# Decode of a down projection's output pair emitted ahead of the next weight block's split

## The chip, the cores and the metric

The kernel runs on one core of a Trainium2 chip. The metric is the device time in microseconds (us) of one execution; lower is better. The core's engines work side by side, each through its own queue in order, and wait for each other through semaphores: TensorE (PE; matmul, with weight loads shown apart as PEld), VectorE (DVE), ScalarE (ACT), GpSimd (POOL) and SyncE (SP, which issues most of the DMAs). Matmuls write to PSUM, which has eight banks of 128 x 512 float32; everything else lies in SBUF.

## The reference

A trunk of two layers on a sequence of 512 tokens with 1024 channels. In each layer a token mixer and cross attention add to the residual x, and then a gated MLP with a causal convolution of width 3 does:

```python
def conv_ffn(h, w_up, conv_w, conv_b, w_down):
    u = h @ w_up
    c = conv_general_dilated(u, conv_w[:, None, :], window_strides=(1,),
                             padding=[(CONV_WIDTH - 1, 0)], ...) + conv_b
    a, g = jnp.split(c, 2, axis=-1)
    return (jax.nn.silu(g) * a) @ w_down

x = x + conv_ffn(rms_norm(x, ffn_norm[i]), w_up[i], conv_w[i], conv_b[i], w_down[i])
```

The inner width is 2816. Everything is float32. The change is in the last product, `@ w_down`, and in the addition of its result to x.

## The kernel before

Activations are kept transposed: x is eight tiles `xT[0..7]` of 128 channels x 512 tokens. To keep float32 accuracy with fast matmuls, each operand is split into a high part (a cast, on ACT) and a low part (the rest, a subtraction on DVE), and each product is three matmuls: high x high, high x low, low x high.

The MLP of a layer runs in three parts of 4, 4 and 3 inner pairs (`HALVES`); an inner pair is 256 of the 2816 inner channels. Each part first makes its inner activations ("up": matmul, convolution, gate) and then calls `down`, which adds the part's contribution to x. Output channels are handled in four output pairs c = 0..3 of 2 x 128 channels, so c holds `xT[2c]` and `xT[2c+1]`.

In `down`, most products go by Strassen's scheme in Winograd's form: a 2 x 2 block product is made of seven half-size products in place of eight. `seven(c, m)` emits the seven products for output pair c and inner pair m, 21 matmuls of 128 x 256 (L1358). They accumulate over m in four PSUM banks of pair c (`banks[c]`). After the last m, `decode(c)` adds the banks up in the right combination and adds them to x: one copy on ACT (L1368) and seven additions on DVE (L1369 to L1374, L1376). With four inner pairs the order of PE's work is c,m = (0,0) (0,1) (0,2) (1,0) (1,1) (0,3) (1,2) (1,3), then all of c = 2, then all of c = 3. Since PSUM has eight banks and a pair takes four, c = 2 takes over the banks of c = 0, and c = 3 those of c = 1. PE cannot start a bank before decode has read it.

Weights arrive by DMA in blocks of 128 x 1024 into three `raw` buffers. A block for the seven products carries weights for two inner pairs. POOL makes four sums of its quarters in a `wsum` tile (L285, `block_sums`; two such tiles). `combined` then splits both: ACT casts the raw part (L308) and the sums (L311), DVE makes their low parts (L309 and L312). The split block lies in two buffers each of `whi` and `wlo`, of which there are six each, so three such blocks are alive at a time. Blocks of ordinary products are split in L257 and L260.

Who asks for the next block: `emitted(c, m)` (L1347) is called when PE's matmuls of (c, m) have been emitted. After each odd m the block of that pair is done with: `release` counts its buffers as free and `refill` makes the next blocks in the plan of all weights, at most two pieces ahead (a piece is the weights of one output pair, or one half of an up projection). `make_block` emits the split, the POOL sums of the block after it and the DMA of a later one. So the last `emitted` of a pair, at m = nq - 1, emits a split, and `decode(c)` is called right after it.

PE runs in the order in which the code emits. The other engines are ordered by the framework's planner: it simulates the program with costs of its own and lets each engine take the earliest emitted instruction that is ready in its simulation. The order it finds is then fixed, and on the chip each engine's queue runs in that order. `tc.issue_after(ins)` ties what is emitted inside it: each instruction on the engine of `ins` is put behind `ins` in that engine's queue.

Of the kernel before, what the change touches and what calls it, by code (L numbers as in the profile page):

```python
# [85 lines left out]
def _pieces():  # L86
# [3 lines left out]
    def piece(key, name, i, ks, *ranges):  # L90
        plan.append((key, name, i, ks, ranges))

    for l in range(2):
# [24 lines left out]
        for nq in HALVES:  # L118
            for q in range(base, base + nq):
                for key, c in ((("ua", l, q), 256 * q), (("ug", l, q), DFF + 256 * q)):  # L120
                    piece(key, "w_up", l, (6, 7, 4, 5, 0, 1, 2, 3) if key in SEVEN else K8, (c, c + 256))
            for c in range(4):
# [14 lines left out]
    return out  # L137


SEVEN = [("ua", l, q) for l in range(2) for q in (5, 6, 8, 9)] + [("ug", 0, 9)]  # L140
SUMS_AT = {1:(4,5),2:(0,1),3:(2,3)}
TURNS = ('mm', 'mm', 'sm', 'sm', 'lg', 'lg', 'tp', 'tp')

# [41 lines left out]
def trunk(ctx, tc, head_d, x_t, mem_t, wpack, cols_a_d, cols_d, conv_d, gate_d, rel_bias, diff_lambda, consts, onehot, out):  # L185
    nc = tc.nc
    mm = nc.tensor.matmul
    V, A, G = nc.vector, nc.scalar, nc.gpsimd
# [9 lines left out]
    def bank(tag):  # L198
        return ps.tile([128, 512], F32, name=f"ps_{tag}", tag=tag)
# [12 lines left out]
    def blk(b, w=128):  # L212
        return slice(w * b, w * b + w)
# [108 lines left out]
    def by_seven(i):  # L322
        return plan[i][0][0] == "dn" or plan[i][0] in SEVEN

# [76 lines left out]
    def product(p, parts, n, pairs, ids=None, total=None):  # L401
        ids = range(len(parts)) if ids is None else ids
        total = len(parts) if total is None else total
        first, last = (ids[0], ids[-1]) if len(ids) == total else (0, total - 1)
        for i in ids:
            (hi, lo), (bh, bl) = parts[i], pairs[i]
            mm(p, hi[:, blk(n)], bh, start=i == first, stop=False)  # L407
            mm(p, hi[:, blk(n)], bl, start=False, stop=False)  # L408
            mm(p, lo[:, blk(n)], bh, start=False, stop=i == last)  # L409
# [65 lines left out]
    first = [bank("mm"), bank("mm"), bank("sm"), bank("sm")]  # L475
# [25 lines left out]
    with tc.tile_pool(name="ini", bufs=1) as ip, tc.manual_schedule(engines={E.Activation, E.DVE, E.Pool, E.SP}):  # L501
# [57 lines left out]
        for k in range(KT):  # L559
# [19 lines left out]
            full, left, right = slice(0, S), blk(0, S // 2), blk(1, S // 2)  # L579
# [588 lines left out]
    def ffn(pool, l, acc):  # L1168
# [5 lines left out]
        left, right = blk(0, 256), blk(1, 256)  # L1174

        def take(n):
            nb[0] += n
            return [bank(TURNS[i % 8]) for i in range(nb[0] - n, nb[0])]

        def refill():  # L1180
            nonlocal live
            while done[0] < min(len(order), first_of[min(used[0] + 2, len(plan))]) and live + sizes[done[0]] <= WB:
                live += sizes[done[0]]
                make_block()

        def begin(key):
            nonlocal live
            assert plan[used[0]][0] == key, (plan[used[0]][0], key)
            used[0] += 1
            refill()  # L1190
            return used[0] - 1

        def whole_piece(i):
            nonlocal live
            while done[0] < first_of[i + 1]:
                live += sizes[done[0]]
                make_block()
            assert live <= WB
            return made[i]

        def release(i, n, all_of_it=False):
            nonlocal live
            live -= n
            if all_of_it:
                made[i] = None
            refill()

        def ctile():
            return pool.tile([128, S], F32, name="cvo", bufs=7)
# [64 lines left out]
        def mid_tile():  # L1274
            return xs.tile([128, S], F32R, name="mid", tag="xs", bufs=XS)
# [62 lines left out]
        def down(base, nq, mids, pairs, last, acc2):  # L1338
            first = used[0]
            whole = [plan[first + c][0][0] == "dw" for c in range(4)]  # L1340
            banks, seen = {}, [set() for _ in range(4)]

            def start(c):
                begin(("dw" if whole[c] else "dn", l, base, c))
                banks[c] = take(2 if whole[c] else 4)

            def emitted(c, m):  # L1347
                if m == nq - 1 or m % 2:
                    release(first + c, 1 if whole[c] else 2, m == nq - 1)

            def seven(c, m, some=steps):
                while len(made) <= first + c or len(made[first + c]) <= m:
                    refill()
                for i in some:
                    b, h = place[i]
                    (hi, lo), (bh, bl) = made[first + c][m][i], mids[m][i]
                    for t, (w, v) in enumerate(((hi, bh), (hi, bl), (lo, bh))):
                        mm(banks[c][b][:, h], w, v, start=b not in seen[c], stop=m == nq - 1 and t == 2 and i in close)  # L1358
                        seen[c].add(b)
                if some[-1] != steps[-1]:  # L1360
                    return
                emitted(c, m)
                if m == nq - 1:
                    decode(c)

            def decode(c):
                b, x1, x2, u, y = banks[c], xT[2 * c], xT[2 * c + 1], ctile(), ctile()[:, left]
                A.copy(u[:, left], b[2][:, left])  # L1368
                V.tensor_add(x1, x1, b[0])  # L1369
                V.tensor_add(y, u[:, left], b[2][:, right])  # L1370
                V.tensor_add(u[:, right], y, b[1][:, right])
                V.tensor_add(y, y, b[3][:, left])
                V.tensor_add(x2, x2, b[1])
                V.tensor_add(x1, x1, u)  # L1374
                x2v = x2.rearrange("p (h c) -> p h c", h=2)
                V.tensor_add(x2v, x2v, y.unsqueeze(1).to_broadcast([128, 2, 256]))  # L1376
                if last and l == 1:
                    for n in (2 * c, 2 * c + 1):
                        nc.sync.dma_start(out[n], xT[n])

            def eight(c, n, m0, m1, total=nq):
                parts = whole_piece(first + c)
                product(banks[c][n], parts, n, pairs, range(2 * m0, 2 * m1), 2 * total)

            if all(whole):
                for c0 in (0, 2):
                    cs = (c0, c0 + 1)
                    for c in cs:
                        start(c)
                        for n in range(2):  # L1390
                            eight(c, n, 0, nq - 1)
                        emitted(c, 1)
                    for c in cs:
                        for n in range(2):
                            eight(c, n, nq - 1, nq)
                            update(2 * c + n, banks[c][n], lambda k: c_attn(1, k), acc2)
                            nc.sync.dma_start(xres[2 * c + n], xT[2 * c + n])
                        emitted(c, nq - 1)
                return
            own, mixed = steps[:3], steps[3:]  # L1400
            seq = [(0, m, steps) for m in range(nq - 1)] + [(1, 0, steps)]
            if nq > 3:
                seq += [(1, 1, steps), (0, nq - 1, steps)] + [(1, m, steps) for m in range(2, nq)]
            else:
                seq += [(0, nq - 1, own), (1, 1, own), (0, nq - 1, mixed), (1, 1, mixed), (1, 2, steps)]
            seq += [(c, m, steps) for c in ((2,) if whole[3] else (2, 3)) for m in range(nq)]
            for c, m, some in seq:
                if c not in banks:
                    start(c)
                seven(c, m, some)  # L1410
            if whole[3]:
                start(3)
                eight(3, 0, 0, nq)
                V.tensor_add(xT[6], xT[6], banks[3][0])
                nc.sync.dma_start(out[6], xT[6])
                eight(3, 1, 0, nq - 1, nq - 1)
                V.tensor_add(xT[7], xT[7], banks[3][1])
                for t, p, queue in zip((left, right), take(2), (nc.sync, nc.scalar)):
                    p = p[:, :S // 2]
                    parts = made[first + 3]  # L1420
                    product(p, parts[-2:], 1, [(bh[:, t], bl[:, t]) for bh, bl in pairs[-2:]])
                    V.tensor_add(xT[7][:, t], xT[7][:, t], p)
                    queue.dma_start(out[7, :, t], xT[7][:, t])

        base, acc2 = 0, None
        for part, nq in enumerate(HALVES):
            mids, pairs = [], []
            last = part == len(HALVES) - 1
            for q in range(base, base + nq):
                c2, ops, at, cs = [], [], {}, {}  # L1430

                def half(key, n, j):
                    if n == 0:
                        at[key] = begin((key, l, q))
                        if (key, l, q) in SEVEN:
                            cs[key] = [conv(p, j + i) for i, p in enumerate(up_by_seven(at[key]))]
# [5 lines left out]
                for n in range(2):  # L1442
                    ua = half("ua", n, 2 * q)
                    ug = half("ug", n, 22 + 2 * q)
# [11 lines left out]
                    else:  # L1456
                        m = mid_tile()
# [104 lines left out]
```

## Time and profile before

| | |
|---|---|
| median of 3 runs | 1151.06 us (1149.73 to 1151.46) |
| the profiled execution | 1149.61 us, of it the span 1147.8 us |
| PE busy | 1139.8 us (99% of the span) |
| DVE, ACT, POOL busy | 932.1, 618.8, 279.3 us |
| granted TensorE clock | 1.000 |
| steps of decode: L1368 / L1369 / L1376 | 19 times each; 373, 676 and 685 ns (median) |

The span is the time from the first to the last instruction; the rest of the profiled time lies around it. Matmuls are pipelined and their ends are modelled, so a busy PE is not PE at its peak: whether PE lost time is read from the starts of its matmuls. A row of the timeline gives start, duration, engine, line, operation, output tile <- input tiles, shapes and the count; in square brackets stands how long the engine was idle before it, and what ended that wait.

### The profile page before, as it was taken

The page shows a single profiled execution, that of the slowest core. Times are in us where ns is not written, and L with a number is a line of the kernel's source. Part 1 is how long each engine was busy: PE and PEld are TensorE (multiplying, and loading weights), DVE is VectorE, ACT ScalarE, POOL GpSimd, SP SyncE. Part 2 cuts the span into 40 slices and gives each one's busy share as a digit, 9 for nine tenths or more (in the row PEclk, how much of TensorE's full clock was granted, in tenths as well). Part 3 has the DMA queues.
Part 4 walks back from the last instruction along what each step waited for, and adds up shares of the span by engine and source line. Part 5 has one row for each costly group of instructions (what it writes and reads, how often), then busy time and mean ns, then how long its engine had stood idle before and what let it go on. Part 6 is the DMA issues. An engine that isn't in the chain of part 4 may idle for free.

```text
span 1147.8 us, 17525 instructions
## 1 busy us (share of the span) xinstructions
PE 1139.8 (99%) x6554; PEld 993.0 (87%) x6554; DVE 932.1 (81%) x1553; ACT 618.8 (54%) x1097; POOL 279.3 (24%) x326
## 2 busy tenths in 40 slices
PE   9999999999999999999999999999999999999998
PEld 7888888888899888999888888988888989899888
DVE  8576778689998899899777637777898888989987
ACT  6676686556553355444557634535655435544542
POOL 0000000004374425760000000000246432575240
PEclk9999999999999999999999999999999999999999
DMA  8522242133314332343252230334222343234312
GB/s 297 166 78 91 79 142 70 60 110 91 111 57 131 108 92 75 92 129 111 87 180 71 96 99 11 96 126 123 74 89 77 94 128 92 91 93 129 107 50 101
DMA packets 39666, 117.87 MB, mean 103 GB/s; under 512 B 4767, under 2 KB 7256, under 8 KB 39582
## 3 DMA queue, kind: packets, MB, share of 16 engines
q1 hardware_dynamic: 39150, 116.37, 32.7%
q8 instruction: 51, 0.84, 0.3%
q10 hardware_dynamic: 432, 0.39, 0.1%
q14 instruction: 33, 0.27, 0.1%
HBM read 112.54 MB, written 4.21 MB: 102 GB/s over the span
## 4 chain that ended last, share of the span: by engine, by line
PE 95%; POOL 2%; DVE 1%; ACT 1%; issue 1%; DMA 0%; SPq 0%; POOLq 0%; ACTq 0%
PE ps_mm L407 6%; PE ps_mm L408 6%; PE ps_mm L409 6%; PE ps_mm L385 6%; PE ps_mm L387 6%; PE ps_mm L386 6%; PE ps_sm L408 4%; PE ps_sm L409 4%; PE ps_sm L407 4%; PE ps_lg L1358 4%; PE ps_mm L1358 3%; PE ps_tp L1358 3%; PE ps_tp L224 3%; PE ps_lg L1233 3%; PE ps_tp L408 3%; PE ps_tp L407 3%
## 5 line engine op out<-in xcount | busy, mean ns | idle before, releaser
L260 DVE TENSOR_TENSOR wlo<-raw,whi 128x1024 fp32r<-128x1024 f32 (+5 forms) x165 | 185.8, 1137 | 75.3 <-ACT whi L257 73.6
L257 ACT CAST whi<-raw 128x1024 fp32r<-128x1024 f32 (+5 forms) x165 | 157.0, 967 | 103.0 <-PE ps_mm L408 20.2
L285 POOL TENSOR_TENSOR wsum<-raw 128x256 f32<-128x256 f32 (+1 forms) x112 | 99.5, 909 | 119.9 <-DMA raw<-in_wpack_dram 71.6
L385 PE MATMUL ps_mm<-whi,xsh 128*128 128x512 f32 (+2 forms) x328 | 126.2, 385 | 0.0
L387 PE MATMUL ps_mm<-whi,xsl 128*128 128x512 f32 (+2 forms) x328 | 123.0, 375 | 0.0
L386 PE MATMUL ps_mm<-wlo,xsh 128*128 128x512 f32 (+2 forms) x328 | 122.8, 374 | 0.0
L407 PE MATMUL ps_mm<-xsh,whi 128*128 128x512 f32 x294 | 115.5, 393 | 0.0
L408 PE MATMUL ps_mm<-xsl,whi 128*128 128x512 f32 x294 | 114.6, 390 | 0.0
L409 PE MATMUL ps_mm<-xsh,wlo 128*128 128x512 f32 x294 | 114.5, 389 | 0.0
L312 DVE TENSOR_TENSOR wlo<-wsum,whi 128x1024 fp32r<-128x1024 f32 (+1 forms) x56 | 69.0, 1232 | 15.2 <-ACT whi L311 15.0
L1286 POOL TENSOR_TENSOR cvo<-cvo 128x256 f32<-128x256 f32 x56 | 47.4, 865 | 134.5 <-DVE cvo L1450 133.4
L407 PE MATMUL ps_sm<-xsh,whi 128*128 128x512 f32 x202 | 78.6, 389 | 0.0
L408 PE MATMUL ps_sm<-xsl,whi 128*128 128x512 f32 x202 | 78.6, 389 | 0.0
L409 PE MATMUL ps_sm<-xsh,wlo 128*128 128x512 f32 x202 | 78.6, 389 | 0.0
L311 ACT CAST whi<-wsum 128x1024 fp32r<-128x1024 f32 (+1 forms) x56 | 53.5, 956 | 36.5 <-POOL wsum L285 29.5
L385 PEld LDWEIGHTS ps_mm<-whi,xsh 128*128 128x128 f32 x328 | 61.7, 188 | 11.4 <-issue 1.0
L387 PEld LDWEIGHTS ps_mm<-whi,xsl 128*128 128x128 f32 x328 | 61.7, 188 | 11.3
L386 PEld LDWEIGHTS ps_mm<-wlo,xsh 128*128 128x128 f32 x328 | 61.8, 188 | 10.1
L1263 POOL MEMSET xsh<- 128x128 f32 x2 | 0.4, 210 | 276.4 <-PE ps_sm L408 190.1
L409 PEld LDWEIGHTS ps_mm<-xsh,wlo 128*128 128x128 f32 x294 | 55.2, 188 | 11.6
L407 PEld LDWEIGHTS ps_mm<-xsh,whi 128*128 128x128 f32 x294 | 55.2, 188 | 11.3 <-issue 0.3
L408 PEld LDWEIGHTS ps_mm<-xsl,whi 128*128 128x128 f32 x294 | 55.3, 188 | 11.2 <-DVE xsl L366 0.4
(446 smaller groups left out, 3167.8 us busy)
## 6 DMA issues: line engine op xcount, KB each, us to landing
raw<-in_wpack_dram SPq DMA_DIRECT2D x178, 512.0 KB, 3.6
xt<-in_x_t_dram SPq DMA_DIRECT2D x15, 256.0 KB, 5.2
raw<-in_wpack_dram SPq DMA_DIRECT2D x15, 256.0 KB, 2.9
raw<-in_wpack_dram SPq DMA_DIRECT2D x8, 384.0 KB, 3.4
xres<-xt SPq DMA_DIRECT2D x8, 256.0 KB, 3.3
xt<-xres SPq DMA_DIRECT2D x8, 256.0 KB, 6.8
out_dram<-xt SPq DMA_DIRECT2D x7, 256.0 KB, 2.0
bt<-bias_d SPq DMA_DIRECT2D x6, 256.0 KB, 4.0
```

Source lines behind the costliest of these rows:

```text
L257: ins = A.copy(hi[:, c], raw[:, c])
L260: V.tensor_sub(lo[:, c], raw[:, c], hi[:, c].bitcast(F32))
L285: tc.keep_in_program_order(getattr(G, "tensor_" + op)(o, x, y))
L311: A.copy(h1[:, m], wsum[:, m])
L312: V.tensor_sub(l1[:, m], wsum[:, m], h1[:, m].bitcast(F32))
L385: mm(p, sh[k][:, blk(b)], hi, start=k == 0, stop=False)
L386: mm(p, sh[k][:, blk(b)], lo, start=False, stop=False)
L387: mm(p, sl[k][:, blk(b)], hi, start=False, stop=k == KT - 1)
L407: mm(p, hi[:, blk(n)], bh, start=i == first, stop=False)
L408: mm(p, hi[:, blk(n)], bl, start=False, stop=False)
L409: mm(p, lo[:, blk(n)], bh, start=False, stop=i == last)
L1358: mm(banks[c][b][:, h], w, v, start=b not in seen[c], stop=m == nq - 1 and t == 2 and i in close)
```

## The change

In the last step of an output pair (m = nq - 1), in the parts that are not the layer's last, `decode(c)` is emitted first, and `emitted(c, m)` after it. What `emitted` puts on ACT is tied behind the first copy of decode, and what it puts on DVE behind decode's last addition. This concerns the parts with four inner pairs, two in each layer, with four decodes each: 16 decodes. The third decode-using place, the last part of the second layer, keeps its order. `SEVEN`, a list of keys made by a comprehension, is written out as a tuple with the same nine keys.

```diff
-SEVEN = [("ua", l, q) for l in range(2) for q in (5, 6, 8, 9)] + [("ug", 0, 9)]
+SEVEN = (('ua', 0, 5), ('ua', 0, 6), ('ua', 0, 8), ('ua', 0, 9), ('ua', 1, 5), ('ua', 1, 6), ('ua', 1, 8), ('ua', 1, 9), ('ug', 0, 9))
...
                 if some[-1] != steps[-1]:
                     return
-                emitted(c, m)
-                if m == nq - 1:
-                    decode(c)
+                if m < nq - 1 or last:
+                    emitted(c, m)
+                    if m == nq - 1:
+                        decode(c)
+                    return
+                with ExitStack() as stack:
+                    for ins in decode(c):
+                        stack.enter_context(tc.issue_after(ins.ins))
+                    emitted(c, m)
 
             def decode(c):
                 b, x1, x2, u, y = banks[c], xT[2 * c], xT[2 * c + 1], ctile(), ctile()[:, left]
-                A.copy(u[:, left], b[2][:, left])
+                first = A.copy(u[:, left], b[2][:, left])
...
-                V.tensor_add(x2v, x2v, y.unsqueeze(1).to_broadcast([128, 2, 256]))
+                final = V.tensor_add(x2v, x2v, y.unsqueeze(1).to_broadcast([128, 2, 256]))
                 if last and l == 1:
                     for n in (2 * c, 2 * c + 1):
                         nc.sync.dma_start(out[n], xT[n])
+                return first, final
```

## The prediction

> **What bounds the kernel now.** I read the page's busy table and chain first, then the waits of TensorE (PE), and then the four down projections that the change touches, engine by engine, in the timeline. The span is 1147.8 us and PE is busy for 1139.8 of it:
>
> ```profile
> PE 1139.8 (99%) x6554; PEld 993.0 (87%) x6554; DVE 932.1 (81%) x1553; ACT 618.8 (54%) x1097; POOL 279.3 (24%) x326
> ...
> PE 95%; POOL 2%; DVE 1%; ACT 1%; issue 1%; DMA 0%; SPq 0%; POOLq 0%; ACTq 0%
> ```
>
> 95% of the chain that ended last is PE. So the time falls only where PE stands still, and what any other engine does costs nothing until PE waits for it. This is who PE waits for:
>
> ```profile
> PE ps_tp L1358 <- DVE cvo L1370: 1.7, 2, 0.8
> PE ps_sm L1358 <- DVE cvo L1370: 1.6, 2, 1.2
> ```
>
> The columns are the total in us, the number of waits and the longest. These are the longest waits of PE, and the only ones after the start of the kernel: four, one in each of the four down projections with four inner pairs, always for L1370, a step of decode on VectorE (DVE). Why DVE is late shows in its timeline in the second of the four (layer 0):
>
> ```profile
> 470.40 1.21 DVE L312 TENSOR_TENSOR wlo<-wsum,whi 128x1024 fp32r<-128x1024 f32 x1
> 471.54 0.94 DVE L309 TENSOR_TENSOR wlo<-raw,whi 128x768 fp32r<-128x768 f32 x1
> 475.71 1.37 DVE L312 TENSOR_TENSOR wlo<-wsum,whi 128x1024 fp32r<-128x1024 f32 x1 [3.23 <-ACT whi L311]
> 477.00 0.41 DVE L1370 TENSOR_TENSOR cvo<-cvo,ps_tp 128x256 f32<-128x256 f32 x1
> ...
> 479.65 1.23 DVE L1376 TENSOR_TENSOR xt<-xt,cvo 128x512 f32<-128x512 f32 x1
> 480.80 1.49 DVE L309 TENSOR_TENSOR wlo<-raw,whi 128x768 fp32r<-128x768 f32 x1
> 482.22 1.76 DVE L312 TENSOR_TENSOR wlo<-wsum,whi 128x1024 fp32r<-128x1024 f32 x1
> 483.91 0.67 DVE L1369 TENSOR_TENSOR xt<-xt,ps_mm 128x512 f32<-128x512 f32 x1
> 484.50 0.41 DVE L1370 TENSOR_TENSOR cvo<-cvo,ps_sm 128x256 f32<-128x256 f32 x1
> ...
> 486.81 0.69 DVE L1376 TENSOR_TENSOR xt<-xt,cvo 128x512 f32<-128x512 f32 x1
> ```
>
> DVE works its queue in order. The split of the next weight block (L309 at 471.54, L312 at 475.71) stands ahead of L1370, and DVE sits idle for 3.23 us before L312, with decode behind it. What L312 waits for, and whether decode was ready, show ScalarE (ACT) and GpSimd (POOL):
>
> ```profile
> 469.92 0.37 ACT L1368 COPY cvo<-ps_tp 128x256 f32<-128x256 f32 x1
> 470.52 0.83 ACT L308 CAST whi<-raw 128x768 fp32r<-128x768 f32 x1 [0.23 <-PE ps_tp L1358]
> 474.63 1.05 ACT L311 CAST whi<-wsum 128x1024 fp32r<-128x1024 f32 x1 [3.27 <-POOL wsum L285]
> 475.58 0.37 ACT L1368 COPY cvo<-ps_sm 128x256 f32<-128x256 f32 x1
> ```
>
> ```profile
> 473.05 0.73 POOL L285 TENSOR_TENSOR wsum<-wsum,raw 128x256 f32<-128x256 f32 x1
> ...
> 475.96 1.71 POOL L285 TENSOR_TENSOR wsum<-wsum,raw 128x256 f32<-128x256 f32 x1
> ```
>
> L312 needs L311, and L311 needs POOL's four sums, which end at about 474.6. Decode's copy (L1368) was over at 470.29. So decode was ready some 7 us before it ran, held by a split that was itself waiting. On PE it looks so:
>
> ```profile
> 476.44 0.28 PE L1358 MATMUL ps_lg<-mid,wlo 128*128 128x256 f32 x1
> 477.56 0.48 PE L1358 MATMUL ps_tp<-mid,whi 128*128 128x256 f32 x2 [0.84 <-DVE cvo L1370]
> 477.87 0.28 PE L1358 MATMUL ps_tp<-mid,wlo 128*128 128x256 f32 x1
> 477.99 0.40 PE L1358 MATMUL ps_tp<-mid,whi 128*128 128x256 f32 x2
> 478.22 0.28 PE L1358 MATMUL ps_tp<-mid,wlo 128*128 128x256 f32 x1
> 478.61 0.47 PE L1358 MATMUL ps_lg<-mid,whi 128*128 128x256 f32 x2
> 478.92 0.28 PE L1358 MATMUL ps_lg<-mid,wlo 128*128 128x256 f32 x1
> ```
>
> and undisturbed, in the chain, nine matmuls take 1.08 us, 0.12 us each from start to start:
>
> ```profile
> 479.56 1.08 PE ps_lg L1358 x9
> ```
>
> **The change part by part.** SEVEN as a tuple holds the same nine keys and is only asked "is this key in it": it emits nothing, 0.
>
> The move itself adds and removes no instruction. It emits the decode of an output pair before the weight block that this pair's last step frees, and ties that block's ACT and DVE instructions behind decode's first copy and last addition. It acts on 4 decodes in each of 4 down projections.
>
> *ACT.* The tie asks for L1368 before the casts. The rows have that order already (L1368 at 469.92, L308 at 470.52): 0.
>
> *DVE, first decode (c = 0).* L1370 to L1376 move ahead of L309 and L312 of the block freed there. They can start when L1368 is over (470.29) and when the earlier block's L312 is off DVE (471.54, where the row of the next instruction starts). (L1369, the first addition, ran before these rows already.) These six take 486.81 + 0.69 - 484.50 = 3.0 us, and 479.65 + 1.23 - 477.00 = 3.88 beside a busy POOL. So they end at 474.5 to 475.4, and PE, which wants the bank at 476.44 + 0.12 = 476.56, finds the whole decode finished; both of its stops here go. Their size: 477.56 - 476.56 = 1.00, then 477.87 - 477.56 - 2 x 0.12 = 0.07, 478.61 - 478.22 - 0.12 = 0.27 (the second bank, which decode reads last in L1373) and 478.92 - 478.61 - 0.24 = 0.07: 1.41 us. In the other three the first stop is
>
> ```profile
> 349.32 0.28 PE L1358 MATMUL ps_mm<-mid,wlo 128*128 128x256 f32 x1
> 349.95 0.35 PE L1358 MATMUL ps_sm<-mid,whi 128*128 128x256 f32 x1 [0.35 <-DVE cvo L1370]
> ...
> 900.41 0.28 PE L1358 MATMUL ps_mm<-mid,wlo 128*128 128x256 f32 x1
> 901.89 0.36 PE L1358 MATMUL ps_sm<-mid,whi 128*128 128x256 f32 x1 [1.20 <-DVE cvo L1370]
> ...
> 1028.38 0.28 PE L1358 MATMUL ps_lg<-mid,wlo 128*128 128x256 f32 x1
> 1029.50 0.36 PE L1358 MATMUL ps_tp<-mid,whi 128*128 128x256 f32 x1 [0.84 <-DVE cvo L1370]
> ```
>
> 0.51, 1.36 and 1.00 by the same subtraction. (The waits put it lower, 0.35 to 1.20, since they count a matmul's modelled end as work; start to start is what the end of the kernel feels.) I take the 0.41 that follows from the case shown for all four. Sum: 1.00 + 0.51 + 1.36 + 1.00 + 4 x 0.41 = 5.5 us.
>
> *What is late next.* The moved split (L309, L312) starts at 474.5 to 475.4 in place of 471.54. L309 takes 0.94 to 1.49, L312 cannot start before L311 ends (475.68) anyway and takes 1.37 to 1.76: it ends at 477.1 to 478.7, before at 477.08. PE needs this block two steps of 21 matmuls (seven products of three) after 476.56, at 476.56 + 42 x 0.12 = 481.6. Cover about 3 us, cost 0. If the cover went, each us beyond it would cost one us in each of the four.
>
> *Second decode (c = 1).* It too goes ahead of a split (that at 480.80). Seven instructions, 483.91 to 487.50, are 3.6 us (4.5 with POOL busy). From 477.1 to 478.7, and not before its copy (475.58 + 0.37), they end at 480.7 to 483.2; the split after them takes 0.94 + 1.37 to 1.49 + 1.76 and ends at 483.0 to 486.4. It is due after 84 matmuls, at 486.6: covered, but at the worst end by 0.2 only.
>
> *Third and fourth decode.* Behind them go splits of the next up projection's weights. When the third decode starts, the fourth pair still takes 84 matmuls (10.1 us), so the 3.6 us of the third are covered. What goes behind the fourth is not the next weight piece but the one after it: 0 as well; uncovered, each would cost at most its 3.6.
>
> *Queues.* Decode issues no DMA in these four, so SP's weight loads keep their order. A weight buffer comes free up to about 3.9 us later (L309 from 471.54 to about 475.4), and so does the load into it; that load serves a block three later, not due in this pair: 0. POOL's sums have no tie. They wait for L312 to free their buffer, which moves by 0 to 1.6 us: under the same covers.
>
> POOL and DVE do get in each other's way: L1376 took 1.23 beside POOL (at 479.65) against 0.69 (at 486.81), and POOL's sums took 1.71 beside DVE against 0.73 with DVE idle. Decode now runs where POOL's sums had DVE idle; two additions from SBUF can hold up the sums by about 2 x 0.7 = 1.4 us. L311 then ends at 477.1, L312 at 478.5 to 478.8: inside the cover of 481.6, but it pushes the second decode's split towards 486.6.
>
> The Trainium skill has a rule that speaks against the move here ("SBUF — State Buffer", section "Who interferes with whom"): a DVE instruction with both inputs in SBUF and a GpSimd instruction that reads SBUF exclude each other for their whole length. The rows agree in kind, but they show a stretch of 0.5 us for L1376 (1.23 against 0.69); by the rule as by the rows the sum stays 5.5, and only the second split's margin suffers.
>
> *The sum.* The profiled execution took 1149.61 us (span 1147.8 and 1.81 around it); less 5.5 it is 1144.1. The median of the runs is 1151.06, 1.45 above it; less 5.5 it is **1145.6 us**, 0.48% less. A change of 0.2% (2.3 us) is about the least that can be told from none.
>
> **The rivals.**
>
> *A new wait at the second split (partial gain).* If POOL's hindrance and the long durations meet, the block due at 486.6 is late by up to 1.4 - 0.2 = 1.2 us in each projection; four such take back up to 4.8 of the 5.5. With half of it, 0.8 each, 3.2 is lost: 1148.8. For it: the worst sum has only 0.2 us. Against it: the short durations leave 3.6.
>
> *Decode is not pulled forward, but the split is pushed back (slower).* The planner that orders ACT, DVE and POOL may leave L1370 to L1376 where they are (477.00 to 480.88), while the tie sends L309 and L312 behind them: L312 ends at 480.88 + 0.94 + 1.37 = 483.2 to 484.1, due at 481.6, so 1.6 to 2.5 us are lost in each besides the old stop: 4 x 2 = 8, 1159. It decides once L1376 ends later than 481.6 - 2.3 = 479.3. Against it: the copy was ready at 470.29 and nothing else stands on DVE between 471.54 and 475.71.
>
> *No change.* PE stops at the same place for something else, such as the first block's split. Its L312 (470.40) is over at 471.6, 5 us before it is due, so I see no candidate: 1151.
>
> **How the numbers follow.** Full gain 0.76 (1145.6); partial 0.08 (1148.8, half of it beyond 0.2%); no change 0.06; slower 0.10 (1159). Faster 0.76 + 0.04 = 0.80, same 0.06 + 0.04 = 0.10, slower 0.10. PE has no other wait to lose, so the low end is the fastest run, 1149.73, less 5.5 and 0.7 for reading errors: 1143.5. The high end takes in the partial case with most of its loss, 1150.0. That leaves out the slower case and half of no change.
>
> **What would show it.** Right: no PE wait on L1370 is left, the six decode instructions stand directly behind the L312 near 470 with no idle of 3.2 us before the next L312, and PE's matmuls at the start of the third pair are 0.12 apart. Wrong: PE or its weight loads waiting on L309 or L312 two or four steps later, L1376 ending after the third pair starts, or POOL's sums ending more than 3 us later than now.

## The result, and the profile after

| | before | after |
|---|---|---|
| median of 6 executions | 1150.29 us (1149.54 to 1151.46) | 1144.29 us (1144.10 to 1145.39) |
| the profiled execution | 1149.61 us | 1144.21 us |
| its span | 1147.8 us | 1142.4 us |

The ratio is 0.9948, with a 95% interval of 0.9936 to 0.9961. The kernel became 6.0 us faster by the medians and 5.4 us by the two profiled executions. In the later sessions below, the median of before was 1149.50 to 1149.83 us, so 5.4 is the nearer figure.

The code grew above `decode`, so the line numbers of after are shifted: the copy L1368 is now L1374, the first addition L1369 is L1375, L1370 to L1373 are L1376, L1377, L1378 and L1379, L1374 is L1380, and the last addition L1376 is L1382. L1376 is thus the last step of decode in the rows of before, and the second in the rows of after.

The page of after, with the busy table, the chain that ended last by engine, and one group of instructions (total and mean busy time, then the idle time before them and what ended most of it):

```profile
PE 1137.8 (100%) x6554; PEld 992.9 (87%) x6554; DVE 934.7 (82%) x1553; ACT 619.8 (54%) x1097; POOL 279.5 (24%) x326
...
PE 99%; DMA 0%; DVE 0%; issue 0%; SPq 0%; ACT 0%
...
L312 DVE TENSOR_TENSOR wlo<-wsum,whi 128x1024 fp32r<-128x1024 f32 (+1 forms) x56 | 67.1, 1198 | 7.1 <-ACT whi L311 5.6
```

The last row in the page of before:

```profile
L312 DVE TENSOR_TENSOR wlo<-wsum,whi 128x1024 fp32r<-128x1024 f32 (+1 forms) x56 | 69.0, 1232 | 15.2 <-ACT whi L311 15.0
```

The chain is now 99% PE, and DVE, ACT and POOL, which held 4% of it between them, are down to nothing or nearly so. The instruction counts of all engines are the same as before. DVE's idle time in front of L312 fell from 15.2 to 7.1 us: DVE stands still less in the place where decode was queued behind it. The waits of PE in after (total us, number, longest):

```profile
PE ps_tp L512 <- PEq L1524: 0.8, 1, 0.8
PE ps_mm L586 <- DVE wlo L260: 0.3, 1, 0.3
PE ps_mm L586 <- ACT xsh L365: 0.2, 1, 0.2
```

The four waits for decode (1.7 + 1.6 us) are gone, and nothing has come in their place: these three belong to the start of the kernel. Measured from start to start of PE's matmuls at L1358, before lost 5.50 us and after 0.00.

The same place as in the prediction, the second of the four projections (layer 0), in the timeline of DVE after:

```profile
469.46 1.21 DVE L312 TENSOR_TENSOR wlo<-wsum,whi 128x1024 fp32r<-128x1024 f32 x1
470.60 0.41 DVE L1376 TENSOR_TENSOR cvo<-cvo,ps_tp 128x256 f32<-128x256 f32 x1
...
473.27 1.23 DVE L1382 TENSOR_TENSOR xt<-xt,cvo 128x512 f32<-128x512 f32 x1
474.42 1.49 DVE L309 TENSOR_TENSOR wlo<-raw,whi 128x768 fp32r<-128x768 f32 x1
475.83 1.76 DVE L312 TENSOR_TENSOR wlo<-wsum,whi 128x1024 fp32r<-128x1024 f32 x1
...
480.77 1.22 DVE L1382 TENSOR_TENSOR xt<-xt,cvo 128x512 f32<-128x512 f32 x1
481.92 0.95 DVE L309 TENSOR_TENSOR wlo<-raw,whi 128x768 fp32r<-128x768 f32 x1
482.79 1.21 DVE L312 TENSOR_TENSOR wlo<-wsum,whi 128x1024 fp32r<-128x1024 f32 x1
```

and of PE after:

```profile
475.50 0.28 PE L1358 MATMUL ps_lg<-mid,wlo 128*128 128x256 f32 x1
475.62 0.40 PE L1358 MATMUL ps_tp<-mid,whi 128*128 128x256 f32 x2
```

The decode starts as soon as the L312 of the earlier block is off DVE. It is over at 473.27 + 1.23 = 474.50, and PE takes the bank at 475.62, 0.12 us after the matmul before it. Before, PE wanted the bank at 476.56 and got it at 477.56. (After reaches this place 0.94 us earlier, because the first projection has already gained its 0.51 + 0.41.) No idle time stands in front of the L312 at 475.83.

The sums of POOL, and the cast that needs them, in after:

```profile
468.21 3.07 POOL L285 TENSOR_TENSOR wsum<-raw 128x256 f32<-128x256 f32 x2 [4.96 <-ACT whi L308]
471.24 0.74 POOL L285 TENSOR_TENSOR wsum<-wsum,raw 128x256 f32<-128x256 f32 x1
472.06 0.74 POOL L285 TENSOR_TENSOR wsum<-raw,wsum 128x256 f32<-128x256 f32 x1
```

```profile
472.83 1.05 ACT L311 CAST whi<-wsum 128x1024 fp32r<-128x1024 f32 x1 [2.42 <-POOL wsum L285]
```

The sums still end late, at 472.80, and the cast L311 still waits for them. What has changed is only who stands behind that wait on DVE. Compared queue by queue, the order of the instructions is the same in both kernels on PE, ACT, POOL and SP; only DVE's differs.

### The profile page after: what moved, and what is told of

Its sections match the earlier page's. It is cut to its first block, busy times and chain, and to the rows that moved or that the text cites. A ratio compares the mean times of both kernels' runs of the same rounds, so it can differ in the third digit from the quotient of the medians.

```text
span 1142.4 us, 17519 instructions
## 1 busy us (share of the span) xinstructions
PE 1137.8 (100%) x6554; PEld 992.9 (87%) x6554; DVE 934.7 (82%) x1553; ACT 619.8 (54%) x1097; POOL 279.5 (24%) x326
## 4 chain that ended last, share of the span: by engine, by line
PE 99%; DMA 0%; DVE 0%; issue 0%; SPq 0%; ACT 0%
PE ps_mm L407 6%; PE ps_mm L408 6%; PE ps_mm L409 6%; PE ps_mm L385 6%; PE ps_mm L387 6%; PE ps_mm L386 6%; PE ps_lg L1358 5%; PE ps_sm L407 4%; PE ps_sm L408 4%; PE ps_sm L409 4%; PE ps_mm L1358 4%; PE ps_tp L1358 4%; PE ps_sm L1358 3%; PE ps_tp L224 3%; PE ps_lg L1233 3%; PE ps_tp L408 3%
## 5 line engine op out<-in xcount | busy, mean ns | idle before, releaser
L311 ACT CAST whi<-wsum 128x1024 fp32r<-128x1024 f32 (+1 forms) x56 | 53.6, 957 | 49.3 <-POOL wsum L285 43.7
L1286 POOL TENSOR_TENSOR cvo<-cvo 128x256 f32<-128x256 f32 x56 | 47.4, 866 | 134.3 <-DVE cvo L1457 133.2
L312 DVE TENSOR_TENSOR wlo<-wsum,whi 128x1024 fp32r<-128x1024 f32 (+1 forms) x56 | 67.1, 1198 | 7.1 <-ACT whi L311 5.6
L387 PEld LDWEIGHTS ps_mm<-whi,xsl 128*128 128x128 f32 x328 | 61.7, 188 | 11.3
L407 PEld LDWEIGHTS ps_mm<-xsh,whi 128*128 128x128 f32 x294 | 55.3, 188 | 11.3 <-issue 0.3
```

The source lines that it names most:

```text
L311: A.copy(h1[:, m], wsum[:, m])
L312: V.tensor_sub(l1[:, m], wsum[:, m], h1[:, m].bitcast(F32))
L387: mm(p, sl[k][:, blk(b)], hi, start=False, stop=k == KT - 1)
```

## Experiments

All are compared with the kernel before on the same chip. Line numbers are those of each kernel.

**The first decode alone, and the other three alone.** The theory says that only the decode of the first output pair (c = 0) is worth anything, since PE waits there and nowhere else. The rival is that each of the four decodes brings its part. Two kernels split the change between them.

```diff
-                if m < nq - 1 or last:
+                if m < nq - 1 or last or c != 0:
```

> Only the first decode (c = 0) of each of the four projections is moved and tied; the decodes of c = 1, 2, 3 keep their old place. Theory (the gain is the first decode alone, since only there PE waited): the whole gain, 1144.3 us, ratio to the kernel before 0.995, no PE wait on decode. Rival (each of the four moved decodes brings its part, through buffers that come free earlier): about a quarter of it, 1148.8 us, ratio 0.999.

Measured: 1144.14 us (1144.06 to 1144.43), ratio 0.9952 (0.9938 to 0.9965). This is the whole gain. PE has no wait at L1358 left.

```diff
-                if m < nq - 1 or last:
+                if m < nq - 1 or last or c == 0:
```

> The counterpart: the decodes of c = 1, 2, 3 are moved and tied, the first keeps its old place. Theory: no gain, 1150.3 us, ratio 1.000, and the four PE waits of 0.35 to 1.2 us on L1376 (the renumbered L1370) are all there, behind the idle of about 3.2 us before L312. Rival: three quarters of the gain, 1145.8 us, ratio 0.996.

Measured: 1149.79 us, ratio 1.0000 (0.9992 to 1.0009), the time of before. PE's waits in this kernel are those of before, under the new line number of the same step:

```profile
PE ps_tp L1358 <- DVE cvo L1376: 1.7, 2, 0.9
PE ps_sm L1358 <- DVE cvo L1376: 1.6, 2, 1.2
```

So 4 of the 16 moved decodes carry the gain, and the other 12 are worth nothing that can be measured.

**The order without the tie.** Is it enough to emit decode first, or must the split be tied behind decode's last addition?

```diff
-                with ExitStack() as stack:
-                    for ins in decode(c):
-                        stack.enter_context(tc.issue_after(ins.ins))
-                    emitted(c, m)
+                decode(c)
+                emitted(c, m)
```

> Decode is emitted first as in the change, but nothing is tied behind it. The planner then puts the freed block's L309 between decode's second and third DVE step, and its L312 still behind decode. Theory (what matters is that no waiting L312 stands ahead of decode): the full gain, 1144.3 us, ratio 0.995, since L309 delays the rest of decode by 0.9 to 1.5 us and there are 2 us to spare. Rival (the tie is needed): the old waits are back, 1149 to 1150 us.

Measured: 1143.84 us (1143.61 to 1144.27), ratio 0.9952 (0.9939 to 0.9964). DVE's timeline in the same place:

```profile
470.20 0.41 DVE L1376 TENSOR_TENSOR cvo<-cvo,ps_tp 128x256 f32<-128x256 f32 x1
470.53 1.16 DVE L309 TENSOR_TENSOR wlo<-raw,whi 128x768 fp32r<-128x768 f32 x1
471.61 0.41 DVE L1377 TENSOR_TENSOR cvo<-cvo,ps_lg 128x256 f32<-128x256 f32 x1
...
473.58 1.23 DVE L1382 TENSOR_TENSOR xt<-xt,cvo 128x512 f32<-128x512 f32 x1
474.73 1.76 DVE L312 TENSOR_TENSOR wlo<-wsum,whi 128x1024 fp32r<-128x1024 f32 x1
```

Now L309, which needs no sums, slips in between two steps of decode, but L312, which does, stays behind them. That is enough: the gain comes from decode standing ahead of the one instruction that waits for POOL, not from its standing ahead of the whole split. The tie is not needed here. This kernel, after, and the one with the first decode alone cannot be told apart by their times.

**A later sum, in both kernels.** If before lost its time because decode was queued behind a split that waited for POOL, then sums that end later must cost before the same again, and after nothing. The first sum of the block whose wait holds decode is made three times (with the same result), which adds two sums to POOL in each of the four projections. It is done in the kernel before and in the kernel after.

```diff
-        g_sums((("add", s1, a21, a22), ("sub", s3, a11, a21), ("sub", s2, s1, a11), ("sub", s4, a12, s2)))
+        g_sums((("add", s1, a21, a22),) * (3 if plan[order[done[0]][0]][0][0] == "dn" and plan[order[done[0]][0]][0][3] == 2 and plan[order[done[0]][0]][0][2] < 8 and done[0] - first_of[order[done[0]][0]] == 1 else 1) + (("sub", s3, a11, a21), ("sub", s2, s1, a11), ("sub", s4, a12, s2)))
```

> The kernel before, with the first of POOL's four sums of one block made three times over (the same result): the block whose split stands ahead of the first decode, in each of the four projections. All other queues keep their order. Two more sums of 0.74 to 1.1 us each, so L311 and L312 come 1.5 to 2.2 us later. Theory (the first decode, and PE behind it, hang on these sums): each us of it is lost on PE in each of the four, 6 to 9 us more, 1156 to 1159 us. Rival (POOL's delay is hidden, PE waited for the amount of DVE work): 1150.3 to 1152 us.

> The same two extra sums per projection in the changed kernel. Theory (the first decode no longer hangs on POOL; the late block has about 2 to 3 us of cover): 1144.3 us, at most 1146, so that the gap to the kernel before with the same extra sums is 12 to 15 us. Rival (the change only moved the wait, its cover is used up already): 6 us or more slower than the changed kernel, 1150 us.

Measured: before with the extra sums takes 1158.33 us (ratio 1.0076, 1.0063 to 1.0090), after with them 1145.76 us (ratio to the plain before 0.9966, 0.9954 to 0.9979). The same work on POOL costs 8.8 us in the one and 1.5 us in the other. PE's waits in before with the extra sums:

```profile
PE ps_tp L1358 <- DVE cvo L1370: 4.6, 2, 2.3
PE ps_sm L1358 <- DVE cvo L1370: 4.5, 2, 2.6
```

Its DVE, in the second projection:

```profile
480.06 1.34 DVE L312 TENSOR_TENSOR wlo<-wsum,whi 128x1024 fp32r<-128x1024 f32 x1 [4.73 <-ACT whi L311]
```

DVE's idle time ahead of L312 grew from 3.23 to 4.73 us, by 1.50. The four stops of PE grew from 0.51, 1.00, 1.36 and 1.00 to 1.99, 2.47, 2.81 and 2.48, by 1.45 to 1.48 each: what POOL is late by goes to PE one for one, through a split that PE does not need yet. These 5.9 us leave 2.9 of the 8.8 open; they are the clock, below. The gap between the two kernels is 12.6 us, as the theory had it (12 to 15). In after with the extra sums, the L312 of the same place waits 0.30 us, decode is long over by then, and no wait for decode appears. Of its 1.5 us, PE shows 1.3 from start to start at L1358. About 0.3 of that is the split of the second decode, whose L312 now ends just too late for the fourth pair in the third and fourth projection (0.1 and 0.2 us), so a little of the rival is true as well. The larger part, 1.0, is one stop elsewhere, in the last part of layer 1:

```profile
PE ps_tp L1358 <- DVE mid L1279: 0.7, 1, 0.7
```

It measures 0.88 us from start to start, and 0.10 more at the next matmul. DVE there runs some 2 us later against PE than in after, and L1279 with it; where DVE first falls behind was not found.

**Where the missing 2.9 us went.** The view of stretches, for the 3 us behind the stops of before with the extra sums. The columns are the stretch, its length, the busy time of PE, PEld, DVE, ACT and POOL, then the granted TensorE clock, the DMA share and the GB/s:

```profile
351.60:355.00 3.40, 3.38 (x16) 3.40 (x17) 3.40 (x6) 1.05 (x1) 3.32 (x5) 0.53 0.01 5
481.80:485.00 3.20, 3.12 (x15) 3.15 (x16) 3.20 (x5) 1.05 (x1) 3.12 (x5) 0.52 0.02 9
908.70:912.00 3.30, 3.24 (x17) 3.27 (x18) 3.30 (x6) 1.05 (x1) 3.22 (x5) 0.57 0.02 9
1038.70:1042.00 3.30, 3.14 (x24) 2.99 (x25) 3.30 (x6) 1.05 (x1) 3.22 (x5) 1.00 0.04 16
```

After three of the four stops the clock was granted at about half for 3 us, and PE did 15 to 17 matmuls in place of 24. After the fourth, which was no shorter (2.48 us), it stayed at 1.00. Does the surplus come from the clock, or does POOL's delay itself cost PE more than it is long? The kernel before with one extra sum in place of two (`* (2 if` in the same line) was to tell.

> The kernel before with one extra sum per projection in place of two. With two, the stops of PE grew from 0.51, 1.00, 1.36, 1.00 us to 1.99, 2.47, 2.81, 2.48, by 1.48 each, but the time grew by 8.8 us and not 5.9; behind three of the four stops the granted TensorE clock stood near one half for some 3 us. Theory A (one for one, and a stop of some 2 us or more can also cost the clock): stops grow by 0.74 each to 1.25, 1.74, 2.10 and 1.74; with the clock unharmed 1152.5 us, with one or two places at the half clock (about 1 us each) 1153.5 to 1154.5. Theory B (the surplus of 2.9 us came from more DVE and POOL work being late, not from the clock): 1154 us with the clock at 1.00 in all four places.

Measured: 1155.64 us (1152.37 to 1157.59), ratio 1.0046 (1.0033 to 1.0059). The stops are 1.34, 1.71, 2.08 and 1.73, on average 0.75 longer than before, about the length of one sum (0.74 us): one for one, as with two. The executions spread over 5 us, and they are ordered by their mean clock: 1152.37 at 1.000, 1154.19 at 0.999, 1155.59 and 1155.69 at 0.997, 1157.15 and 1157.59 at 0.996. The one that kept its full clock took 2.5 us more than before (1149.83), against 0.75 x 4 = 3.0. The rest is the clock. In the profiled execution (1155.69) it fell to one half after two of the four stops, from 905.57 to 908.97 us and from 1035.28 to 1038.68. The rows show the stretches around the second stop (at 479.07, 1.71 us), which kept its clock, and around the third (at 904.18, 2.08 us), which did not:

```profile
475.49:478.89 3.40, 2.02 (x17) 1.82 (x16) 1.66 (x2) 2.05 (x3) 3.40 (x4) 1.00 0.48 148
478.90:482.31 3.41, 3.14 (x24) 2.99 (x25) 3.38 (x7) 1.05 (x1) 3.33 (x5) 1.00 0.02 6
902.16:905.56 3.40, 1.37 (x10) 1.13 (x10) 3.17 (x6) 1.58 (x4) 3.32 (x4) 1.00 0.52 154
905.57:908.97 3.40, 3.40 (x19) 3.40 (x18) 3.40 (x4) 0.62 (x1) 3.32 (x4) 0.50 0.00 0
908.98:912.38 3.40, 3.40 (x30) 3.40 (x30) 3.37 (x5) 1.79 (x2) 0.50 (x1) 1.00 0.48 154
```

1155.69 - 1152.37 = 3.3 us for two such places, about 1.6 each, which is more than the one microsecond I had taken. Counted from start to start within the one execution, they are 1.4 each; with two extra sums they are 1.0 each, since there the slow stretch began while PE still stood. With that the account nearly closes: at L1358 PE loses 14.3 us with two sums, 11.3 with one and 5.5 in before, which is 8.8 and 5.8 more, and the spans of the profiled executions are 9.2 and 6.0 longer. The surplus is thus spent in the slow stretches, as in theory A.

**How much cover the moved split has.** The change pushes the split of the next block behind decode. Extra additions on DVE behind the first decode (`u` added to itself, which nobody reads afterwards) push it further, by two or by five additions of 0.68 to 1.23 us each.

```diff
-                return first, final
+                return first, [final, *(V.tensor_add(u, u, u) for _ in range(2 if not last and c == 0 else 0))][-1]
```

> The changed kernel with two additions on DVE behind the first decode in place of five. The planner lets one step of the second decode go ahead of the tied split as well, so this split comes 1.8 to 2.6 us later, with 2.7 to 3.1 us of cover in the changed kernel; the second decode's split comes 1.2 to 2.0 us later, with about 1.6 us of cover. Theory (these covers, read from the changed kernel's trace, are what there is): no stop at the first split, at the second 0 to 0.4 us in each projection, 1144.3 to 1146 us. Rival (any delay of the splits reaches PE): 4 x 2 us more, 1152 us.

Measured: 1145.99 us (1145.26 to 1146.51), ratio 0.9964 (0.9952 to 0.9976). PE does not stop for the first split. At the second it loses 0.2 us in the second projection and 0.3 in the third from start to start, too little to show among the waits, and within the 0 to 0.4 that was expected. Most of the 1.7 us over after is again in the last part of layer 1, a stop of 1.03 us that after does not have (again put down to L1279), so this run bounds the cover without giving a clean price.

With `range(5 ...)` in the same line:

> The changed kernel with five additions from SBUF to SBUF (0.69 us each, 0.60 from start to start, on a tile that nobody reads again) on DVE behind the first decode and ahead of the split that is tied to it. The planner lets four or five steps of the second decode go ahead of that split too, so it comes 4.7 to 7 us later. In the changed kernel it ends 2.7 to 3.1 us before PE needs it. Theory (that cover is all there is): PE loses 1.8 to 4 us in each of the four, 7 to 16 more, about 1153 us, with PE waiting at the third step of c = 2. Rival (cover is larger since PE waits for something else as well): 1144 to 1147 us.

Measured: 1153.66 us (1153.61 to 1154.51), ratio 1.0038 (1.0025 to 1.0050): slower than before. The largest of PE's waits, and PE's timeline in the second projection:

```profile
PE ps_lg L1358 <- DVE wlo L312: 1.8, 4, 0.5
PE ps_mm L1358 <- DVE wlo L312: 1.8, 4, 0.5
```

```profile
482.89 0.39 PE L1358 MATMUL ps_lg<-mid,wlo 128*128 128x256 f32 x1 [0.44 <-DVE wlo L309]
...
484.02 0.39 PE L1358 MATMUL ps_lg<-mid,wlo 128*128 128x256 f32 x1 [0.52 <-DVE wlo L312]
```

Each projection now stops 1.2 to 1.6 us at its third step and 0.5 at the start of the fourth pair. In all PE loses 9.6 us from start to start (0.6 of it in the last part of layer 1), and 1144.2 + 9.6 = 1153.8 is about the time measured. The cover is real and finite, and the whole gain hangs on it.

**Take the wait away and leave the order.** If the split's wait for the sums is the cause, decode may stay behind it as long as the sums are early. A third `wsum` tile lets POOL make them earlier. Five in place of seven `cvo` buffers make room for it, so there is a control with that alone. Both start from the kernel before, and the order of every queue is the same in the two.

```diff
-            return pool.tile([128, S], F32, name="cvo", bufs=7)
+            return pool.tile([128, S], F32, name="cvo", bufs=5)
```

> Control for the next kernel: the kernel before with five buffers for the decode and convolution tiles (cvo) in place of seven, which makes room in SBUF. The queue orders around decode are those of before. Both theories: the four PE waits on L1370 stay (0.92 to 1.76 us lost in each); the convolutions may wait more for a buffer, 1150 to 1154 us.

Measured: 1161.92 us (1161.08 to 1162.48), ratio 1.0105 (1.0091 to 1.0119), far more than expected. The stops on decode grew to 1.44, 3.02, 3.03 and 3.02 us, and the clock went down to one half behind the second and the third of them. In the second projection, DVE's step L1450, ahead of the inner products, starts 3.2 us later than in before and PE only 1.2 us later; so the whole chain of DVE and POOL arrives 2.0 us later against PE, which is what the stop grew by. What holds DVE up further ahead was not found. The control thus changes more than the room in SBUF.

```diff
-        return sum_pool[0].tile([128, WTILE], F32, name="wsum", bufs=2)
+        return sum_pool[0].tile([128, WTILE], F32, name="wsum", bufs=3)
```

> As the control, with a third tile for POOL's sums (wsum), so that the sums of the late block need not wait for an earlier split to free a tile. Every queue has the same order as in the control, so decode still stands behind L309 and L312. Theory (what cost time was DVE's idle wait for the late sums, with decode behind it, not the split's own 2.3 us of work): L312 starts some 3 us earlier, decode is over before PE wants the bank, 5.5 us faster than the control, ratio 0.995. Rival (the work of the split ahead of decode is what delays it): at most 2 us faster than the control, and PE waits on L1370 stay.

Measured: 1158.04 us (1154.90 to 1159.04), ratio 1.0065 (1.0053 to 1.0078), so 3.9 us below its control by the medians and not the 5.5 expected; its executions spread with the mean clock, 0.998 for the fastest and 0.996 for the slowest. DVE and PE in the first projection of the control

```profile
348.83 1.37 DVE L312 TENSOR_TENSOR wlo<-wsum,whi 128x1024 fp32r<-128x1024 f32 x1 [3.23 <-ACT whi L311]
350.12 0.41 DVE L1370 TENSOR_TENSOR cvo<-cvo,ps_sm 128x256 f32<-128x256 f32 x1
...
350.67 0.48 PE L1358 MATMUL ps_sm<-mid,whi 128*128 128x256 f32 x2 [1.28 <-DVE cvo L1370]
```

and with the third tile:

```profile
347.60 1.21 DVE L312 TENSOR_TENSOR wlo<-wsum,whi 128x1024 fp32r<-128x1024 f32 x1
348.74 0.40 DVE L1370 TENSOR_TENSOR cvo<-cvo,ps_sm 128x256 f32<-128x256 f32 x1
...
349.68 0.40 PE L1358 MATMUL ps_sm<-mid,whi 128*128 128x256 f32 x2
```

The order is the same, the wait is gone, and with it every wait of PE for L1370. In the first projection this confirms the cause: nothing held PE up ahead of this place, and L1370 is over 0.54 us before PE takes the bank. The other three projections prove less. There PE has just stood for 2.2 us at a new wait, and L1370 is over some 0.55 us (in two) and 2.0 us (in one) before PE comes; whether it would have been in time without that stop, these rows do not show. The new wait is also why less time was gained than the wait removed:

```profile
PE ps_tp L1358 <- DVE mid L1279: 4.6, 5, 1.4
PE ps_sm L1358 <- DVE mid L1279: 1.6, 2, 1.1
```

The earlier sums now run beside other work of DVE, the three additions of L1286 just ahead of the projection's inner products:

```profile
466.56 2.61 DVE L1286 TENSOR_TENSOR cvo<-cvo 128x256 f32<-128x256 f32 x3
```

They take 2.61 us; the control's, with a sum beside only the first of them, take 1.51. They stand ahead of the additions (L1279) for which PE then waits. That this collision is the whole of the new wait was not shown. Making the waiting instruction early, rather than moving work past it, left the kernel slower than before; but it came together with the smaller `cvo`, so its own worth is open.

## Why the prediction was right

*The place.* Right. PE's four stops were all there was to win; after has none of them, and the run with the first decode alone has the whole gain.

*The size.* The sum was 5.5 us, with the 0.41 of small stops taken from one projection for all four. Measured: 5.50 us from start to start over all four, 5.4 by the spans. The profiled execution was put at 1144.1 and took 1144.21.

*The step from there to the median.* This is where 1145.6 is 1.3 us too high. I carried over the 1.45 us by which the median of three executions then lay above the profiled one. Over six executions before lies 0.68 above it, and after 0.08. The offset was scatter of a few executions, not a property of the kernel.

*First decode.* It was to end at 474.5 to 475.4 on before's clock. Taking off the 0.94 us by which after is early, this is 473.6 to 474.5; it ended at 474.50, the late end. L1380 and L1382 took 0.96 and 1.23 us beside POOL against 0.69 undisturbed, as the range had it.

*POOL held up by decode.* I allowed for sums that end up to 1.4 us later. They ended at 472.80, in before at 474.60; of the 1.8 us, 0.94 is the shift, so they came 0.9 us earlier instead. In before, the first two took

```profile
469.15 3.93 POOL L285 TENSOR_TENSOR wsum<-raw 128x256 f32<-128x256 f32 x2 [4.96 <-ACT whi L308]
```

and 3.07 in after. In before they ran beside two full-size instructions, L312 and L309; in after L309 came only later. The second sum ended 0.6 us behind L309 in before (473.08 and 472.48) and 0.6 us behind L312 in after (471.28 and 470.67), which is how POOL's sums follow such instructions elsewhere (last section). What decode's last two additions did hold up were the sums of the block after: they end at 478.20, and in before at 478.49, which is 477.55 with the 0.94 taken off, so 0.65 us later. The fear was real but fell on another block, and it touched nothing that PE waits for. The prediction also took the stretch of 0.5 us for less than a shutting out by whole instructions; the rows show that it is one (last section).

*First split.* Its cover was to be about 3 us. It ended at 475.83 + 1.76 = 477.59. The prediction counted the due time from the matmul that stopped, which is the seventh of the third pair. By the trace the third step starts at 479.94, and its sixth matmul, five times 0.12 later, is the first that needs what L312 makes: 480.54, so 2.9 us (2.5, 2.6 and 3.0 in the other projections). That it is cover, and that going beyond it costs PE time, the five extra additions showed.

*Second split.* I gave it 0.2 to 3.6 us. It ended at 482.79 + 1.21 = 484.00, and the sixth matmul of the fourth pair, which starts at 484.98, needs it at 485.58: 1.6 us (1.4, 1.3 and 1.6 in the other projections). The run with two extra additions, which pushed it back by about as much, lost 0.2 and 0.3 us there in two projections. The bad end, on which the partial rival rested, came from adding the long duration of every instruction; they did not all meet POOL.

*The other decodes, ACT's tie, the queues.* All were put at nothing. The three other decodes alone gave a ratio of 1.0000; ACT's, POOL's and SP's queues run in the same order as before.

*The rivals.* No new wait at the second split appeared. The slower rival needed decode to stay where it was in the planner's order while the split moved behind it. In after decode went to 470.60, and even without any tie it stayed ahead of L312. The mechanism behind that rival is nonetheless true: with the split pushed back further, the kernel lost 4.2 us against before. "No change" fell with PE's waits.

## What to carry to other kernels

When PE waits for a short instruction, look on that instruction's engine for an idle gap in front of an earlier instruction in the queue: here decode had its input 7 us before it ran, behind a split that stood waiting for POOL and was itself not needed until 5 us after PE's stop. Moving the ready work ahead of the waiting work was worth PE's stops in those places, and moving it elsewhere was worth nothing. Before moving, count the cover of what is pushed back: here it was 2.5 to 3.0 us for the first split and 1.3 to 1.6 for the second, and five extra additions used it up and turned the gain into a loss.

## What the runs showed of the hardware that I had not expected

**A stop of PE can cost its clock as well.** In before, stops of 0.51 to 1.36 us left the granted clock at 1.00. In the kernels with extra sums and with five `cvo` buffers, stops of 1.73 to 3.03 us were followed by half the clock in seven places, but others of 1.71, 2.48 and 3.02 us were not, and the same kernel lost more or fewer places from one execution to the next (mean clock 1.000 to 0.996, 1152.37 to 1157.59 us). A place costs 1.0 to 1.4 us more from start to start, so a stop near 2 us can cost half as much again as its length, or more.

The traces suggest what decides. The half clock starts and ends on steps of 3.41 us: with one extra sum it starts at 905.57 and 1035.28, 38 such steps apart; with two at 351.78, 481.49 and 908.15, 38 and 125 steps apart. Before each start, PE had stood for 2.03 us or more within one such step, counted from start to start. In every other step of a down projection at full clock it stood for at most 1.88. The three long stops that kept the clock were cut in two by the border of a step: that of 1.71 at 478.90 (1.54 us before it), that of 2.48 at 1037.86 (1.58), that of 3.02 at 1039.89 (1.83). And with the third sums tile two short stops, 0.65 and 1.35 us, fell into one step (2.15 in all) and cost the clock from 1025.93 on. Where the steps lie differs from trace to trace (one starts at 478.90 with one extra sum, at 478.07 with two), which would explain the chance. All this is read from traces made for other ends; no run moved a stop against the steps to test it.

The Trainium skill ("TensorE: Matmul & The Clock Gate", section "What's actually happening") tells of a half clock after an idle window of about 3.4 us, in windows that run freely of the kernel. The rows agree with the half clock, with the length of the window and with its running freely. They differ on how idle it must be: 2.03 us of standing still within a window were enough here.

**Beside POOL, an addition from SBUF waits for the running sum to end.** Against the DVE rows of before in the prediction stand these of POOL:

```profile
478.46 1.88 POOL L285 TENSOR_TENSOR wsum<-raw 128x256 f32<-128x256 f32 x2
480.29 1.19 POOL L285 TENSOR_TENSOR wsum<-wsum,raw 128x256 f32<-128x256 f32 x1
481.56 1.34 POOL L285 TENSOR_TENSOR wsum<-raw,wsum 128x256 f32<-128x256 f32 x1
```

The sums end at 480.34, 481.48 and 482.90. DVE's L1376, L309 and L312 end at 480.88, 482.29 and 483.98: 0.5, 0.8 and 1.1 us behind the sum that ran as they began, not much less than they take undisturbed (0.69, 0.94 and 1.21). POOL's last two sums in turn end 0.6 us behind DVE's L1376 and L309. The two take turns by whole instructions, and how far one is stretched depends on how much of the other was left when it began. In after, all 108 stretched additions and subtractions of these four sizes from SBUF end at such a fixed distance behind an instruction of POOL (0.28 us for 128x256, 0.55 for 128x512, 0.82 for 128x768, 1.08 for 128x1024). Additions that read PSUM were not stretched: L1379 took 0.68 us beside a sum. No such stretch lay on PE's path in after.
